# Moving the parameter work of an S5 branch and the rope table to the head of a fused mixer, and GpSimd's arithmetic there to VectorE

## The chip, the cores and the metric

The kernel runs on one core of a Trainium2 chip. A core has TensorE (PE, matrix products and transposes), VectorE (DVE), ScalarE (ACT), GpSimd (POOL) and the queue engine SyncE (SP), which here issues nearly all loads. The engines run side by side and wait for each other through semaphores. The metric is the device time of one execution in microseconds (us); lower is better.

## The reference

One transformer layer on 512 tokens of width 1024, in float32: a mixer of two branches, a cross attention to a memory, and a mixture of experts with 64 experts. The change is in the mixer alone:

```python
proj = x @ w_in
h_q, h_kv, k_rope_raw, u, g_mla, g_s5 = split(proj)
# S5 branch: per group g (32 groups, 64 states, 16 channels) a diagonal complex recurrence
dt = exp(log_dt); abar = exp(a * dt); bbar = ((abar - 1) / a) * b        # complex, from parameters alone
x_t = abar * x_{t-1} + bbar @ u_t;  y_t = Re(c @ x_t) + d * u_t
y_s5 = val * sigmoid(gate),  val, gate = split(gelu(y) @ w_glu)
# latent attention: q, k, v from rms_norm(h_q), rms_norm(h_kv), rope with cos/sin(positions * inv_freq)
merged = sigmoid(g_mla) * y_mla + sigmoid(g_s5) * y_s5
```

Everything that the S5 branch needs of `a`, `b`, `c` and `log_dt` (powers of `abar`, `bbar`, the step matrices) and the rope table `cs` depends on no product with x.

## The kernel before

float32 products are computed as three products of the engine's rounded float32 form: each operand is split into a high part (a cast by ACT, line 167) and a remainder (a subtraction, line 168, by DVE or by an engine that is passed in), and `mm3` issues high x high, high x low and low x high (L201 to L203). A weight of 128x2048 goes through `load` (a DMA on SP into one of two raw buffers), and `split`. Names: `wu0`, `wu1` are the two halves of u's weight, `wg00` to `wg31` those of the four gate blocks; a trailing r, h or l is the raw, high or low tile.

The front of the kernel, up to the first value product `pvv` of the attention, runs in this order of the code:

- x and `wqkv` are loaded; x is transposed (`xT`) and split; the latents `pl` = x @ wqkv; their mean squares and a Newton iteration on DVE (`ms`, `rms`, L306 and L210 to L219); the scaled latents (`lat`) are transposed (`cT`).
- `pu` = u, then transposed (`uT`). The S5 parameters: `nat`, `ldt`, `braw`, `cn` are loaded, `s5p` transposed, a long chain of small DVE operations on 128x16 tiles (`sp`, `pw`, `ap`, `bb`), the transposes `cstT` and `cst`. The rope table: `posi`, `ang`, `cs`.
- For four quarters Q: `factors` computes the step matrices `wi` on DVE, copied into `bd`, transposed into `im` (`imT`), the product `pkc`, and `pv`. Then the scan `vv` (`advance`, L608 to L611, on DVE), its carry `zz`, `factors` for the output matrices `om` (on POOL), and the correction of `vv` (L641, L642: on DVE, on POOL for Q = 3), then `py`, `yT`.
- Between these, the gate products `pg` run on PE as its filler; then `pq`, `pgl` and `pvv`.

A scheduler orders each engine's instructions by the position in the code, with the gate weights' splits advanced by a fixed offset, and each engine runs its list strictly in that order. Each DMA on SP also waits until the DMA eight places before it has landed, and buffers of one tag (the three `m2` buffers, the two raw weight buffers) are reused in turn.

The places that the change touches read, before:

```python
wu = w_cols(O_U, "wu")                    # the loads of u's weight; behind them, in the code, the loads of nat, ldt, braw, cn
w = factors(Q, 1, cst, -1, f"om{Q}", G)   # G is POOL, V is DVE
E = G if Q == 3 else V
wg = w_cols(c0, f"wg{i}", G if i in (0,3) else V)
G.tensor_copy(z[:, k, :, 96:112], z[:, k, :, 80:96].bitcast(F32))
```

Of the kernel before, what the change touches and what calls it, by code (L numbers as in the profile page):

```python
# [21 lines left out]
P = 128  # L22
# [79 lines left out]
def layer(ctx, tc, x, mem, positions, w_in, q_norm_g, kv_norm_g, w_uq, w_ukv, w_mla_o,  # L102
# [127 lines left out]


# [27 lines left out]
    c2_stack, cf_stack, cq_stack = ExitStack(), ExitStack(), ExitStack()  # L259
    c2p = c2_stack.enter_context(tc.tile_pool(name="c2p", bufs=1, side="right"))  # L260
    cfp = cf_stack.enter_context(tc.tile_pool(name="cfp", bufs=1, side="right"))
    mla = cq_stack.enter_context(tc.tile_pool(name="mla", bufs=1))
    identb = mla.tile([P, P], BF16, name="identb")
    V.tensor_copy(identb, ident)
    causal = mla.tile([P, P], BF16, name="causal")
    G.memset(causal, 0.0)
    G.affine_select(out=causal, in_=causal, compare_op=OP.is_ge, fill=-BIG, base=0,
                    pattern=[[-1, P]], channel_multiplier=1)

# [3 lines left out]
    rows = cfp.tile([P, 512], F32, tag="m2", bufs=3, name="rows")[:20, :P]  # L273
    r0 = 0
    COL = {}
    for nm, a in (("q", q_norm_g), ("kv", kv_norm_g), ("mg", mem_ln_g), ("mb", mem_ln_b)):
        n = a.shape[1] // P
        nc.sync.dma_start(rows[r0:r0 + n, :], a[0].rearrange("(r c) -> r c", c=P))
        COL[nm] = r0
        r0 += n  # L280
# [10 lines left out]
    wq = []
    for q_, r in enumerate(wqr):
        h, l = hilo(f"wqkv{q_}", (4, 512))
        split(h, l, r)
        wq.append((h, l))
    ssq = const.tile([P, NT, 2], F32, name="ssq")
    pls = four("pl")
    project(wq, pls, lambda i, k, h, l: (xh[:, k, cols_of(i)], xl[:, k, cols_of(i)]), whole)
    for t in range(NT):
        pl = pls[t]  # L300
        c = cfp.tile([P, 512], F32, tag="m2", bufs=3, name=f"lat{t}")
        for j in range(2):
            S.activation(c[:, j * 256:(j + 1) * 256], pl[:, j * 256:(j + 1) * 256], AF.Square,
                         accum_out=ssq[:, t, j:j + 1])
        ms = const.tile([P, 2], F32, tag="ms", bufs=2, name=f"ms{t}")
        V.tensor_scalar(ms, ssq[:, t, :], 1.0 / 256, None, OP.mult)  # L306
        rs = rsqrt(f"rms{t}", ms, RMS_EPS)
        for j in range(2):
            S.activation(c[:, j * 256:(j + 1) * 256], pl[:, j * 256:(j + 1) * 256], AF.Copy, scale=rs[:, j:j + 1])
        tp = trp(f"cT{t}")  # L310
        for k in range(4):
            PE.transpose(tp[:, k * P:(k + 1) * P], c[:, k * P:(k + 1) * P], ident)
        for k in range(4):
            g = col("q", k) if k < 2 else col("kv", k - 2)
            S.activation(cf[:, k, cols_of(t)], tp[:, cols_of(k)], AF.Copy, scale=g)

    s5k = ExitStack()
    s5 = s5k.enter_context(tc.tile_pool(name="s5", bufs=1))


    ujs = s5.tile([P, 2 * GI, STEP, 16], F32, tag="uy", name="ujs")
    wu = w_cols(O_U, "wu")
# [69 lines left out]
    tmpc = s5.tile([P, 4 * GI * 2], F32, name="tmpc")  # L392
# [113 lines left out]
    krr = load(w_inv[:, :, O_KR:O_KR + ROPE], "krr", (KD, ROPE))  # L506
    krw = ring.tile([P, 2048], F32R, tag="whi", bufs=2, name="krw")[:, :KD * P].rearrange("p (a b) -> p a b", a=KD)
    split(krw[:, :, 64:96], krw[:, :, 0:32], krr)
    for a, b in ((96, 80), (112, 64), (32, 16), (48, 0)):
        V.tensor_copy(krw[:, :, a:a + 16], krw[:, :, b:b + 16].bitcast(F32))  # L510
    pk = aux("pk")
    for k in range(KD):
        PE.matmul(pk, krw[:, k, :], xh[:, k, :], start=(k == 0), stop=False)
        PE.matmul(pk, krw[:, k, :], xl[:, k, :], start=False, stop=(k == KD - 1))
    kr = mla.tile([P, T], F32, name="kr")
    kr2 = cfp.tile([P, T], F32, tag="m2", bufs=3, name="kr2")
    S.copy(kr[h64], pk[0:64])
    V.tensor_tensor(kr[h64], pk[h64], kr[h64], OP.add)
    V.tensor_tensor(kr[h64], kr[h64], cs[h64], OP.mult)
    S.copy(kr2[64:96], kr[96:128])  # L520
    S.copy(kr2[96:128], kr[64:96])
    V.tensor_tensor(kr[h64], kr[h64], kr2[h64], OP.add)
    dump("kr", kr[h64])
# [32 lines left out]
    for Q in range(4):  # L556
# [30 lines left out]

        for c in range(2):
# [6 lines left out]
    tpz = s5.tile([P, 1024], F32, tag="tpz", name="tpz")  # L595
    zz = s5.tile([P, 2, GI, NJ], F32, name="zz")
# [24 lines left out]
    ys = s5.tile([P, STEP, 2 * GI, 16], F32, tag="uy", name="ys")  # L621
    pys = []
    for Q in range(4):
        qs = slice(Q * QG, (Q + 1) * QG)

        w = factors(Q, 1, cst, -1, f"om{Q}", G)
        om = ims[Q].rearrange("p c g (b s h) -> p c g b s h", b=2, h=16)
        for b, r in enumerate(halves):
            for c in range(2):
                (S.copy if b else G.tensor_copy)(om[r, c, :, b], w[r, c])  # L630
    for Q in (3, 0, 1, 2):
        qs = slice(Q * QG, (Q + 1) * QG)
        E = G if Q == 3 else V
        f = (bd.rearrange("p a b c d e -> p (a b c d e)") if Q == 3 else tpz)[:, :QG * NJ * n1]
# [1239 lines left out]
```

## Time and profile before

| | us |
|---|---|
| median of 3 runs | 1239.87 (1239.36 to 1240.43) |
| profiled execution | 1243.18, of which the span 1241.4 |
| PE busy | 1177.9 (95% of the span) |
| DVE busy | 900.2 (73%) |
| ACT busy | 726.6 (59%) |
| POOL busy | 329.3 (27%) |
| first `pvv` on PE | 244.09 after the span's start |

A row of the trace has a start or a count, the engine, the line of the kernel, the operation, its output and inputs, and durations; in square brackets or behind `<-` stands what the engine waited for before it. The profiled execution is 3.3 us above the median of the runs; a difference worked out on its rows is taken off the median.

### The profile page before, as it was taken

To read this page: it belongs to the slowest core of one execution; us is meant where nothing else is said; L and a number is where in the kernel's file an instruction comes from. 1 tells how busy PE (TensorE), PEld (TensorE's weight loads), DVE (VectorE), ACT (ScalarE), POOL (GpSimd) and SP (SyncE) were. 2 spreads that over 40 slices of the span, in tenths; PEclk is the share of its full clock that TensorE was granted. 3 is DMA by queue.
4 is the path that set the end of the run, shared out by engine and by line. 5 is a ranking of instruction groups with operands and counts; after the bars stand their busy time and mean duration, and the time that the engine had idled before them with its cause. 6 is when DMAs were issued, how large, how long until landed. Compare 5 with 4: busy or idle time off the path is not lost. (4 is left out here: it accounts for less than half of the span.)

```text
span 1241.4 us, 16244 instructions
## 1 busy us (share of the span) xinstructions
PE 1177.9 (95%) x5556; PEld 847.2 (68%) x5556; DVE 900.2 (73%) x1654; ACT 726.6 (59%) x1221; POOL 329.3 (27%) x280
## 2 busy tenths in 40 slices
PE   7979977899999899999999999999999999999995
PEld 6968866666678787846666666666666666666663
DVE  4588898446756854677778778788787887876785
ACT  3435413544525444424677777777777777776774
POOL 1020735230011243022122322224243232423321
PEclk9989988899999999999999999999999999999998
DMA  6522121121233257347999999999999999999975
GB/s 212 153 77 74 39 94 51 53 68 34 69 136 102 92 188 271 138 183 273 330 366 357 352 370 356 362 357 356 361 365 362 339 366 355 364 357 354 362 257 136
DMA packets 77596, 294.59 MB, mean 237 GB/s; under 512 B 18574, under 2 KB 22722, under 8 KB 52937
## 3 DMA queue, kind: packets, MB, share of 16 engines
q1 hardware_dynamic: 61592, 252.85, 55.1%
q0 software_dynamic: 15920, 40.69, 13.3%
q8 instruction: 44, 0.72, 0.2%
q14 instruction: 40, 0.32, 0.1%
HBM read 276.88 MB, written 32.77 MB: 249 GB/s over the span
## 5 line engine op out<-in xcount | busy, mean ns | idle before, releaser
L1252 POOL DMA_INDIRECT xg<-x2d,idx x64 | 74.0, 1157 | 384.9 <-PE xgT L1270 327.7
L1319 POOL DMA_INDIRECT ysum<-y,idx x62 | 123.1, 1985 | 91.2 <-ACT y L1331 63.2
L201 PE MATMUL pd<-edhl,hTh 128*96 128x512 f32 x124 | 98.4, 794 | 0.0
L1331 ACT ACTIVATE y<-pd,ws 96x512 f32<-96x512 f32 x124 | 78.6, 685 | 9.1 <-PE pd L203 9.1
L1314 PE MATMUL pd<-ed,hT 128*96 128x512 f32 x152 | 77.7, 593 | 0.5 <-PE psd L1531 0.5
L167 ACT CAST xgh<-xgT 128x384 fp32r<-128x384 f32 x128 | 60.3, 480 | 28.7 <-PE xgT L1270 28.6
L1270 PEld LDWEIGHTS xgT<-ident,xg 96*128 96x128 f32 x512 | 70.1, 215 | 7.0 <-issue 1.6
L1270 PE MATMUL xgT<-ident,xg 96*128 96x96 f32 x512 | 72.3, 283 | 1.9 <-DMA xg<-x2d,idx 1.4
L168 DVE TENSOR_TENSOR xgl<-xgT,xgh 128x384 fp32r<-128x384 f32 x128 | 65.0, 548 | 3.6 <-ACT xgh L167 3.6
L167 ACT CAST hTh<-hT 128x96 fp32r<-128x96 f32 x62 | 14.7, 238 | 73.3 <-PE hT L1293 73.3
L168 DVE TENSOR_TENSOR edhl<-ed,edhl 128x1024 fp32r<-128x1024 f32 x38 | 46.4, 1222 | 15.4 <-ACT edhl L167 15.3
L203 PE MATMUL pd<-edhl,hTl 128*96 128x512 f32 x124 | 49.4, 399 | 0.0
L1314 PE MATMUL pd<-edgx,hT 128*96 128x512 f32 x96 | 49.1, 592 | 0.0
L202 PE MATMUL pd<-edhl,hTh 128*96 128x512 f32 x124 | 48.6, 392 | 0.0
L202 PEld LDWEIGHTS pd<-edhl,hTh 128*96 128x96 f32 x124 | 20.2, 163 | 33.0 <-issue 33.0
L201 PEld LDWEIGHTS pd<-edhl,hTh 128*96 128x96 f32 x124 | 20.1, 162 | 33.0 <-issue 33.0
L167 ACT CAST edhl<-ed 128x1024 fp32r<-128x1024 f32 x38 | 39.4, 1037 | 3.8 <-DVE eg11l L168 3.8
L1228 DVE TENSOR_TENSOR oneh<-iota,posh 128x512 f16<-128x512 f16 x64 | 40.4, 681 | 0.1
L168 DVE TENSOR_TENSOR edhl<-edgx,edhl 128x1024 fp32r<-128x1024 f32 x24 | 29.3, 1222 | 10.7 <-ACT edhl L167 10.7
L1303 ACT COPY hT<-hT 128x96 f32<-128x96 f32 x62 | 14.8, 238 | 36.7 <-DVE hTl L168 36.7
L737 DVE TENSOR_REDUCE sm<-ps 128x1 f32<-128x128 f32 (+3 forms) x32 | 15.6, 488 | 23.8 <-PE ps L750 23.1
L665 ACT ACTIVATE sg<-pg 128x512 f32<-128x512 f32 x16 | 9.5, 596 | 36.6 <-PE pg L203 36.5
(1761 smaller groups left out, 3713.4 us busy)
## 6 DMA issues: line engine op xcount, KB each, us to landing
ed<-in_w_exp_down_dram SPq DMA_DIRECT2D x39, 1024.0 KB, 20.4
edgx<-in_w_exp_down_dram SPq DMA_DIRECT2D x25, 1024.0 KB, 13.7
x<-in_x_dram SPq DMA_DIRECT2D x4, 512.0 KB, 7.9
wqkvr<-in_w_in_dram SPq DMA_DIRECT2D x2, 1024.0 KB, 8.6
ysum<-zero SPq DMA_DIRECT2D x1, 2048.0 KB, 10.2
xr<-in_x_dram POOLq DMA_DIRECT2D x4, 512.0 KB, 5.0
wxv<-in_w_xkv_dram SPq DMA_DIRECT2D x2, 1024.0 KB, 6.5
eg3z<-in_w_exp_gu_dram SPq DMA_DIRECT2D x2, 1024.0 KB
```

Source lines behind the costliest of these rows:

```text
L167: a = S.copy(h, src)
L168: b = (eng or V).tensor_tensor(l, src, h.bitcast(F32), OP.subtract)
L201: PE.matmul(o, lh, rh, start=start, stop=False)
L202: PE.matmul(o, lh, rl, start=False, stop=False)
L203: PE.matmul(o, ll, rh, start=False, stop=stop)
L737: V.tensor_reduce(st[:, 0:1], ps, AX.X, OP.max)
L1228: V.tensor_tensor(oh_, iota.unsqueeze(1).to_broadcast([P, NT, P]), posn.to_broadcast([P, NT, P]), OP.is_equal)
L1252: return G.indirect_dma_start(out=xg, out_offset=None, in_=x2d[:, :], in_offset=bass.IndirectOffsetOnAxis(ap=ix, axis=0), bounds_check=T - ...
L1270: m_ = PE.transpose(tp[:, k * CAP:(k + 1) * CAP], xg[:CAP, 512 * z + k:512 * (z + 1):4], ident[:CAP, :CAP])
L1314: PE.matmul(po, f, wf[:, 0, c], start=True, stop=False)
L1319: marks["scatter"] = G.indirect_dma_start(out=ya[:, :], out_offset=bass.IndirectOffsetOnAxis(ap=ix, axis=0), in_=y, in_offset=None, bounds ...
L1331: S.activation(o, po, AF.Copy, scale=w)
```

## The change

Three things, all ahead of `pvv`:

- The loads of the S5 parameters and of the positions go right behind those of x and wqkv, ahead of u's weight. The parameters' arithmetic, the rope table and the step matrices `wi`, `imT`, `pkc` stand in the code ahead of u, the parameters and the rope table even ahead of the latents.
- POOL's arithmetic in the front goes to DVE: the low parts of wg0 and wg3, `om` and its copies, the correction for Q = 3 (which now comes last instead of first) and eight casts of `wuq`. POOL keeps memsets there.
- Pools and tags move with it (`cn` and `tpz` share the tag of `bd`, `im0` and `im1` get tiles of their own, `vv`, `U` and `ys` a new pool).

```diff
+    rows = cfp.tile([P, 512], F32, tag="m2", bufs=3, name="rows")[:20, :P]
...
+    nat = s5.tile([P, 4, P], F32, tag="fac", name="nat")[:GI]
+    nc.sync.dma_start(nat[:, 0, :], s5_a_re[0].rearrange("(a b) p -> a (b p)", b=2))
...
+    nc.sync.dma_start(braw[:, 0], s5_b_re[0].rearrange("(a b) p h -> (b p) a h", b=2))
+    nc.sync.dma_start(braw[:, 1], s5_b_im[0].rearrange("(a b) p h -> (b p) a h", b=2))
+    cns = []
...
+        nc.sync.dma_start(cn[:, :, 0, :], v)
...
+    nc.sync.dma_start(posi[h64], positions[0:1, :].to_broadcast([64, T]))
     xh = Halves(keep, "big", "xh")
...
-    cf = cfp.tile([P, 4, T], F32, name="cf")
...
-    wu = w_cols(O_U, "wu")
...
     S.activation(cs[h64], ang[h64], AF.Sin)
     dump("cs", cs[h64])
+    cf = cfp.tile([P, 4, T], F32, name="cf")
...
+    wu = w_cols(O_U, "wu")
...
+    for Q in range(4):
+        qs = slice(Q * QG, (Q + 1) * QG)
+        w = factors(Q, 0, bb, 1, f"wi{Q}", V)
...
+    pu = four("pu")
+    project(wu, pu, lambda i, k, h, l: (xh[:, k, i::STEP], xl[:, k, i::STEP]), whole)
...
-        w = factors(Q, 1, cst, -1, f"om{Q}", G)
+        w = factors(Q, 1, cst, -1, f"om{Q}", V)
...
-                (S.copy if b else G.tensor_copy)(om[r, c, :, b], w[r, c])
-    for Q in (3, 0, 1, 2):
+                (S.copy if b else V.tensor_copy)(om[r, c, :, b], w[r, c])
+    for Q in range(4):
...
-        E = G if Q == 3 else V
+        E = V
...
-            wg = w_cols(c0, f"wg{i}", G if i in (0,3) else V)
+            wg = w_cols(c0, f"wg{i}", V)
...
-            G.tensor_copy(z[:, k, :, 96:112], z[:, k, :, 80:96].bitcast(F32))
-            G.tensor_copy(z[:, k, :, 112:128], z[:, k, :, 64:80].bitcast(F32))
+            V.tensor_copy(z[:, k, :, 96:112], z[:, k, :, 80:96].bitcast(F32))
+            V.tensor_copy(z[:, k, :, 112:128], z[:, k, :, 64:80].bitcast(F32))
```

SP, from the last load of wqkv's small companions to the first gate weight, before (`ysum` is a 2 MB fill with zeros of a buffer that the experts add into; `krr` the weight of the rope key):

```order
L278 DMA rows<-in_mem_ln_b_dram 8x128
L156 DMA wu0r<-in_w_in_dram 128x4x512
L156 DMA wu1r<-in_w_in_dram 128x4x512
L333 DMA nat<-in_s_a_re_dram 16x128
L334 DMA nat<-in_s_a_im_dram 16x128
L336 DMA ldt<-in_s_log_dt_dram 16x2
L426 DMA braw<-in_s_b_re_dram 128x16x16
L427 DMA braw<-in_s_b_im_dram 128x16x16
L442 DMA cn_554<-in_s_c_re_dram 128x4x64
L799 DMA ysum_1839<-zero 4096x1x128
L156 DMA krr<-in_w_in_dram 128x8x32
L156 DMA wg00r<-in_w_in_dram 128x4x512
```

The same stretch of SP in the changed kernel:

```order
L278 DMA rows<-in_mem_ln_b_dram 8x128
...
L273 DMA braw<-in_s_b_re_dram 128x16x16
L274 DMA braw<-in_s_b_im_dram 128x16x16
L281 DMA cn<-in_s_c_re_dram 128x4x64
L281 DMA cn<-in_s_c_im_dram 128x4x64
L285 DMA posi<-in_positions_dram 64x512
L808 DMA ysum_1842<-zero 4096x1x128
L156 DMA wu0r<-in_w_in_dram 128x4x512
L156 DMA wu1r<-in_w_in_dram 128x4x512
L156 DMA krr<-in_w_in_dram 128x8x32
L156 DMA wg00r<-in_w_in_dram 128x4x512
```

The two loads of u's weight now stand behind the parameters, the positions and the 2 MB fill, which kept its place relative to the parameters.

DVE around the low part of u's first weight half and the first iteration on the latents' mean squares, before:

```order
L337 COPY nat<-ldt 16x128
L168 TENSOR_TENSOR wu0l<-wu0r,wu0h 128x2048
L306 TENSOR_SCALAR ms_290<-ssq 128x2
L443 COPY cn_554<-cn_554 128x4x64
L306 TENSOR_SCALAR ms_319<-ssq 128x2
L210 TENSOR_SCALAR rms_292<-ms_290 128x2
L210 TENSOR_SCALAR rms_321<-ms_319 128x2
```

The same place in the changed kernel, down to the same first step of the iteration:

```order
L168 TENSOR_TENSOR wu0l<-wu0r,wu0h 128x2048
L332 COPY sp<-s5p 128x48
L428 TENSOR_SCALAR cst<-cstT_323 64x256 x2
...
L428 TENSOR_SCALAR cst<-cstT_331 64x256 x2
...
L455 CAST ang<-posi 64x512
L336 TENSOR_SCALAR sp<-sp 128x16
L460 TENSOR_SCALAR phase<-rope_cols 128x1
L483 TENSOR_SCALAR ms_498<-ssq 128x2
L456 TENSOR_SCALAR ang<-ang,rope_cols 64x512
L337 SCALAR_TENSOR_TENSOR sp<-sp 128x16
L210 TENSOR_SCALAR rms_500<-ms_498 128x2
```

Between the split of wu0 and the end of that iteration (`rms_500`) there now stand the parameters' first chain and the rope table's operations, one between the other; before, the split was followed by the iteration alone.

DVE at the end of the correction of `vv`, where `yTz` is the split of the transposed S5 output, before:

```order
L641 TENSOR_TENSOR tpz<-ap,zz 128x448
L642 TENSOR_TENSOR vv<-vv,tpz 128x4x112
L168 TENSOR_TENSOR wukvl<-wukv,wukvh 128x512 x4
L168 TENSOR_TENSOR yTz_1739<-yT_1740,yTz_1738 128x8x16
L168 TENSOR_TENSOR yTz_1739<-yT_1753,yTz_1738 128x8x16
```

The same in the changed kernel:

```order
L650 TENSOR_TENSOR tpz<-ap,zz 128x448
L651 TENSOR_TENSOR vv<-vv,tpz 128x4x112
L168 TENSOR_TENSOR wukvl<-wukv,wukvh 128x512
L168 TENSOR_TENSOR yTz_1741<-yT_1742,yTz_1740 128x8x16
L650 TENSOR_TENSOR tpz<-ap,zz 128x448
L168 TENSOR_TENSOR yTz_1741<-yT_1755,yTz_1740 128x8x16
L168 TENSOR_TENSOR yTz_1741<-yT_1742,yTz_1740 128x8x16
L651 TENSOR_TENSOR vv<-vv,tpz 128x4x112
```

The correction of the last quarter now alternates with the splits of the first quarters' outputs on DVE, where before all of DVE's corrections were done when these began.

## Rows read from the trace of the kernel before

**Rows 1.** The page's head.
```profile
span 1241.4 us, 16244 instructions
```

**Rows 2.** What PE waited for from 0 to 262 us: line, releaser, us in total, times, longest.
```profile
PE pg L203 <- DVE wg21l L168: 9.0, 1, 9.0
PE py L650 <- DVE vv L642: 6.7, 2, 6.2
PE uT L469 <- DVE cst L449: 6.0, 1, 6.0
...
PE yT L674 <- DVE yTz L168: 3.4, 1, 3.4
PE pq L201 <- ACT cT L167: 1.4, 1, 1.4
PE uT L469 <- DVE U L470: 1.1, 1, 1.1
PE pq L202 <- DVE cT L168: 0.9, 1, 0.9
```

**Rows 3.** Stretches of the span: its limits and length, busy us of PE, PEld, DVE, ACT and POOL (with instructions), the granted TensorE clock as a share of full speed, the DMA engines' busy share, GB/s.
```profile
70.00:80.00 10.00, 2.84 (x11) 2.29 (x11) 9.36 (x18) 1.51 (x3) 4.79 (x2) 0.71 0.65 210
80.00:90.00 10.00, 10.00 (x38) 7.85 (x37) 7.92 (x44) 1.22 (x2) 0.00 (x0) 0.78 0.08 29
160.00:170.00 10.00, 6.56 (x23) 5.32 (x24) 9.83 (x13) 0.60 (x1) 0.63 (x1) 0.69 0.54 181
190.00:200.00 10.00, 6.77 (x33) 5.93 (x33) 9.69 (x11) 0.60 (x1) 8.00 (x8) 0.66 0.00 0
220.00:230.00 10.00, 6.87 (x19) 5.12 (x20) 6.09 (x10) 6.52 (x12) 1.73 (x3) 0.54 0.01 2
700.00:800.00 100.00, 100.00 (x477) 67.91 (x475) 80.06 (x106) 76.70 (x122) 25.20 (x20) 1.00 1.02 365
```

**Rows 4.** PE in order of time: start, us, line, operation.
```profile
37.78 0.60 PE L201 MATMUL pu<-wu0h,xhz 128*128 128x512 f32 x1
...
244.09 0.39 PE L201 MATMUL pvv<-wukvh,cT 128*128 128x512 f32 x1
```

**Rows 5.** POOL in order of time: start, us, line, operation, and in brackets its idle time before it.
```profile
70.27 4.52 POOL L168 TENSOR_TENSOR wg01l<-wg01r,wg01h 128x2048 fp32r<-128x2048 f32 x1
...
155.74 4.89 POOL L168 TENSOR_TENSOR wg30l<-wg30r,wg30h 128x2048 fp32r<-128x2048 f32 x1 [2.66 <-ACT wg30h L167]
```

**Rows 6.** DVE in order of time, beside these.
```profile
70.38 4.44 DVE L325 TENSOR_SCALAR sp<-sp 128x16 f32<-128x16 f32 x1
...
156.20 4.98 DVE L610 TENSOR_TENSOR tpz<-tpz,vv 128x512 f32<-128x512 f32 x1
161.10 2.28 DVE L168 TENSOR_TENSOR wg21l<-wg21r,wg21h 128x2048 fp32r<-128x2048 f32 x1
...
195.19 0.63 DVE L641 TENSOR_TENSOR tpz<-ap,zz 128x448 f32<-128x448 f32 x1
```

**Rows 7.** DVE from 60 to 211 us, grouped by line and shape: count, busy us, mean ns of one, idle before.
```profile
L610 DVE TENSOR_TENSOR tpz<-tpz,vv 128x512 f32<-128x512 f32 x7 | 12.7, 1810 | 0.0
L642 DVE TENSOR_TENSOR vv<-vv,tpz 128x448 f32<-128x448 f32 x12 | 9.8, 816 | 0.3
L641 DVE TENSOR_TENSOR tpz<-ap,zz 128x448 f32<-128x448 f32 x12 | 9.8, 813 | 0.4
L608 DVE TENSOR_TENSOR tpz<-ap,vv 128x512 f32<-128x512 f32 x7 | 8.7, 1238 | 0.2
...
L608 DVE TENSOR_TENSOR tpz<-ap,zz 128x32 f32<-128x32 f32 x14 | 7.3, 521 | 0.5
...
L611 DVE TENSOR_TENSOR zz<-tpz 128x32 f32<-128x32 f32 x14 | 3.0, 216 | 0.5
...
L329 DVE SCALAR_TENSOR_TENSOR ang<-posi,ang 64x512 f32<-64x512 f32 x3 | 2.1, 685 | 0.1
...
L549 DVE TENSOR_TENSOR wi<-pw,bb 128x256 f32<-128x256 f32 x4 | 1.7, 422 | 1.1 <-ACT bd L562 1.1
...
L357 DVE SCALAR_TENSOR_TENSOR sp<-sp 128x16 f32<-128x16 f32 x6 | 1.0, 175 | 0.1
```

**Rows 8.** SP's DMA issues in order of time: start, us of issuing.
```profile
12.96 0.41 SPq L156 DMA_DIRECT2D wu0r<-in_w_in_dram  x1
...
30.53 0.65 SPq L799 DMA_DIRECT2D ysum<-zero  x1
32.81 3.97 SPq L156 DMA_DIRECT2D krr<-in_w_in_dram  x1
```

**Rows 9.** DMA issues up to 60 us: count, KB each, median us from issue to landing.
```profile
ysum<-zero SPq DMA_DIRECT2D x1, 2048.0 KB, 10.2
wu0r<-in_w_in_dram SPq DMA_DIRECT2D x1, 1024.0 KB, 5.2
...
krr<-in_w_in_dram SPq DMA_DIRECT2D x1, 128.0 KB, 8.3
```

**Rows 10.** Two short stretches, columns as in Rows 3: the first lies on the parameter loads (64 byte pieces), the second on the fill with zeros.
```profile
28.00:31.50 3.50, 3.50 (x17) 2.89 (x16) 2.43 (x5) 2.64 (x5) 1.38 (x5) 1.00 0.83 96
31.50:35.00 3.50, 3.50 (x17) 2.89 (x16) 3.50 (x23) 0.94 (x5) 0.00 (x0) 1.00 1.00 275
```

**Rows 11.** ACT at the last cast of the latents' weight: start, us, and in brackets what it waited for.
```profile
13.65 1.90 ACT L167 CAST wqkv1h<-wqkvr 128x2048 fp32r<-128x2048 f32 x1 [2.07 <-DMA wqkvr<-in_w_in_dram]
```

More of the change, by code (lines that the diff above doesn't have):

```diff
@@ L229, in layer @@
     G.memset(one1, 1.0)
+    c2_stack, cf_stack, cq_stack = ExitStack(), ExitStack(), ExitStack()
+    c2p = c2_stack.enter_context(tc.tile_pool(name="c2p", bufs=1, side="right"))
+    cfp = cf_stack.enter_context(tc.tile_pool(name="cfp", bufs=1, side="right"))
+    mla = cq_stack.enter_context(tc.tile_pool(name="mla", bufs=1))
+    identb = mla.tile([P, P], BF16, name="identb")
+    V.tensor_copy(identb, ident)
+    causal = mla.tile([P, P], BF16, name="causal")
+    G.memset(causal, 0.0)
+    G.affine_select(out=causal, in_=causal, compare_op=OP.is_ge, fill=-BIG, base=0,
+                    pattern=[[-1, P]], channel_multiplier=1)
+    s5k = ExitStack()
+    s5 = s5k.enter_context(tc.tile_pool(name="s5", bufs=1))
     mix_stack = ExitStack()
@@ L257, in w_cols @@
         return [weight(w_inv[:, 4 * q:4 * q + 4, c0:c0 + 512], f"{name}{q}", (4, 512), None, eng) for q in range(2)]
[L259 to L268, printed above, removed]
     def c2(name, dt=F32):
         return c2p.tile([P, T], dt, tag="c2", bufs=16, name=name)
[L273 to L280, printed above, removed]
+    s5u = s5k.enter_context(tc.tile_pool(name="s5u", bufs=1))
     tp = trp("rowst")
@@ L287, in col @@
         return cols[:, COL[nm] + k:COL[nm] + k + 1]
-    cf = cfp.tile([P, 4, T], F32, name="cf")
[L291 to L321, printed above, removed]
-    wu = w_cols(O_U, "wu")
     def reduce_angle(ang, k, turn):
@@ L390, in layer @@
     V.tensor_tensor(q(CO_I), q(T1), q(DEN), OP.mult)
[L392 removed]
+    tmp3 = s5.tile([P, GI * 16], F32, name="tmp3")
+    tmpc = tmp3
     def cmul(eng, o_r, o_i, a_r, a_i, b_r, b_i, shape, t):
@@ L503, in layer @@
     dump("cs", cs[h64])
[L506 to L523, printed above, removed]
+    cf = cfp.tile([P, 4, T], F32, name="cf")
+    wq = []
+    for q_, r in enumerate(wqr):
+        h, l = hilo(f"wqkv{q_}", (4, 512))
+        split(h, l, r)
+        wq.append((h, l))
@@ new lines, in layer @@
+    ssq = const.tile([P, NT, 2], F32, name="ssq")
+    pls = four("pl")
+    project(wq, pls, lambda i, k, h, l: (xh[:, k, cols_of(i)], xl[:, k, cols_of(i)]), whole)
+    for t in range(NT):
+        pl = pls[t]
+        c = cfp.tile([P, 512], F32, tag="m2", bufs=3, name=f"lat{t}")
+        for j in range(2):
+            S.activation(c[:, j * 256:(j + 1) * 256], pl[:, j * 256:(j + 1) * 256], AF.Square,
+                         accum_out=ssq[:, t, j:j + 1])
+        ms = const.tile([P, 2], F32, tag="ms", bufs=2, name=f"ms{t}")
+        V.tensor_scalar(ms, ssq[:, t, :], 1.0 / 256, None, OP.mult)
+        rs = rsqrt(f"rms{t}", ms, RMS_EPS)
+        for j in range(2):
+            S.activation(c[:, j * 256:(j + 1) * 256], pl[:, j * 256:(j + 1) * 256], AF.Copy, scale=rs[:, j:j + 1])
+        tp = trp(f"cT{t}")
+        for k in range(4):
+            PE.transpose(tp[:, k * P:(k + 1) * P], c[:, k * P:(k + 1) * P], ident)
+        for k in range(4):
+            g = col("q", k) if k < 2 else col("kv", k - 2)
+            S.activation(cf[:, k, cols_of(t)], tp[:, cols_of(k)], AF.Copy, scale=g)
@@ L586, in layer @@
                 nc.sync.dma_start(tzs[Q][b * 64 + sh:b * 64 + 64, b, s_], ks[b * 64:b * 64 + 64 - sh])
+    pu = four("pu")
+    project(wu, pu, lambda i, k, h, l: (xh[:, k, i::STEP], xl[:, k, i::STEP]), whole)
+    for s in range(STEP):
+        S.copy(ujs[:, :, STEP - 1 - s, :], pu[s].rearrange("p (g h) -> p g h", h=16))
+    U = s5u.tile([P, GI, NI, NJ], F32, name="U")
+    for n in range(4):
+        tp = trp(f"uT{n}")
+        for k in range(4):
+            gi = 4 * n + k
+            PE.transpose(tp[:, k * P:(k + 1) * P], ujs[:, 2 * gi:2 * gi + 2].rearrange("p a b c -> p (a b c)"), ident)
+        (S.copy if n % 2 else V.tensor_copy)(U[:, 4 * n:4 * n + 4].rearrange("p a i j -> p a j i"),
+                                             tp.rearrange("p (a j i) -> p a j i", a=4, i=NI))
+    krr = load(w_inv[:, :, O_KR:O_KR + ROPE], "krr", (KD, ROPE))
+    krw = ring.tile([P, 2048], F32R, tag="whi", bufs=2, name="krw")[:, :KD * P].rearrange("p (a b) -> p a b", a=KD)
+    split(krw[:, :, 64:96], krw[:, :, 0:32], krr)
+    for a, b in ((96, 80), (112, 64), (32, 16), (48, 0)):
+        V.tensor_copy(krw[:, :, a:a + 16], krw[:, :, b:b + 16].bitcast(F32))
+    pk = aux("pk")
+    for k in range(KD):
+        PE.matmul(pk, krw[:, k, :], xh[:, k, :], start=(k == 0), stop=False)
+        PE.matmul(pk, krw[:, k, :], xl[:, k, :], start=False, stop=(k == KD - 1))
+    kr = mla.tile([P, T], F32, name="kr")
+    kr2 = cfp.tile([P, T], F32, tag="m2", bufs=3, name="kr2")
+    S.copy(kr[h64], pk[0:64])
+    V.tensor_tensor(kr[h64], pk[h64], kr[h64], OP.add)
+    V.tensor_tensor(kr[h64], kr[h64], cs[h64], OP.mult)
+    S.copy(kr2[64:96], kr[96:128])
+    S.copy(kr2[96:128], kr[64:96])
+    V.tensor_tensor(kr[h64], kr[h64], kr2[h64], OP.add)
+    dump("kr", kr[h64])
+    vv = s5u.tile([P, 2, GI, NI + 1, NJ], F32, name="vv")
+    V.memset(vv[:, :, :, 0, :], 0.0)
+    for Q in range(4):
+        qs = slice(Q * QG, (Q + 1) * QG)
         for c in range(2):
```

63 lines of the change are left out of this document (27 added, 36 removed).

## The prediction

> **What bounds the kernel now.** I read the page's span first (1241.4 us [rows 1], the profiled execution 1243.18 us), then stretches of the span, PE's waits, and DVE and POOL beside each other. From 600 us to the end of the experts PE has no gap: 700 to 800 us shows 100.00 us busy at the full clock, with the DMA engines full too, 365 GB/s [rows 3]. The change touches nothing there, and PE's and ACT's lists from `pvv` on are the same in both kernels; so what the front saves, up to the first `pvv` at 244.09 us [rows 4], the end gets, unless the experts' weights can't come sooner (a rival below).
>
> In the front PE's gaps of over half a microsecond lie in three places and a tail [rows 2]: 6.0 + 1.1 us for `uT` (on `cst`, and `U` behind it), 9.0 us for wg21's low part, 6.7 us for `vv` at `py`, and then 3.4 + 1.4 + 0.9 us for `yT` and `pq`. All of them wait for DVE or what hangs on it. Behind each gap PE runs at the lower granted clock (1.2 of 2.4 GHz) for a while; the stretches show what that costs. Busy time times what the mean clock lacks to 1.00 is 2.84 x 0.29 + 10 x 0.22 = 3.0 us behind the first, 6.56 x 0.31 = 2.0 behind the second, 6.77 x 0.34 = 2.3 behind the third and 6.87 x 0.46 = 3.2 in the tail [rows 3]. So the three gaps cost 10.1 + 11.0 + 9.0 = 30.1 us, the tail 8.9.
>
> **Why DVE is late there.** While POOL subtracts wg01 (70.27 us, 4.52 long [rows 5]), a DVE operation on 128x16 takes 4.44 us, beginning 0.11 us behind it [rows 6]; its like takes 0.175 [rows 7]. While POOL subtracts wg30 (155.74, 4.89), a 512 wide product takes 4.98 [rows 5, 6]. That operation stands right ahead of the split of wg21 (161.10), for which PE waits. The 512 wide operations should cost what L329's cost, 0.685 us, and the 128x32 ones 0.216 [rows 7]. What they took beyond that: L610 12.7 - 7 x 0.685 = 7.9, L608 8.7 - 4.8 = 3.9, L608 on 128x32 7.3 - 14 x 0.216 = 4.3, L641 and L642 9.8 - 12 x 0.63 = 2.2 each, L325 4.3: together 24.8 us of DVE lost to POOL's arithmetic, in these groups alone.
>
> **POOL's work on DVE.** Four splits of 2.28 [rows 6] = 9.1 us; `om`, four times six operations on 128x256 at 0.42 and two copies of half the partitions, at most 0.42 each [rows 7], = 13.4 us at most; the last correction, eight operations on 128x448 at 0.63 [rows 6], = 5.0; eight casts of 128x128, between 0.175 and 0.42 each [rows 7], 1.4 to 3.4, taken as 1.7 since they are small. Sum 29 us against at least 24.8 saved: DVE's load is about what it was. What changes is where the loss stands: no operation of 0.7 us is stretched to five just when PE needs the next split.
>
> **The three gaps.** With `cst`, the parameters and the step matrices done before u, the first gap has no cause left. The second is one stretched operation (4.98) and a DVE list that was 24.8 us behind; the third the same list and its stretched corrections. I take all three as gone, -30.1 us, and put 1 us for new waits on gate splits in the middle, where DVE is nearly full (9.83 of 10 us in 160 to 170 [rows 3]); bounds 0 and 4.
>
> **The new stall ahead of u.** This is the price. The listing shows u's weight behind the parameter loads, the positions and the 2 MB fill on SP, and the DVE list behind wu0's split filled with the parameters' chain and the rope table before the iteration `rms_500`, without which PE can't begin `cT` and, behind it, `pu`.
> - SP's first `braw` waits for the second half of wqkv, landed at 13.65 [rows 11]. Two `braw` and two `cn`, 131 KB each, in 64 to 256 byte pieces: the stretch on these loads moved 96 GB/s with the engines 0.83 busy [rows 10], so 524 KB take 4.5 us. `posi`: 0.5. Now 18.7.
> - The fill: 2.1 MB at 275 GB/s [rows 10], 7.6 us. Now 26.3.
> - wu0: alone it landed 5.2 us after its issue [rows 9]; at 365 GB/s its bytes are 2.9 us of that. Issued early, its latency lies under the fill: it lands between 29.2 and 31.5, taken as 30.3. Before, it was issued at 12.96 [rows 8] and landed at 18.2, long before its cast.
> - ACT's cast 1.9 [rows 11], DVE's split 2.28: 34.5.
> - Then DVE's list to the end of `rms_500`: some 57 operations on 128x16 and less at 0.175 busy, which overlap where two chains alternate (taken as 0.12, 6.8 us; all in a row 10), ten on 64x512 (0.685 for L329's three, less for the simpler: 5 us, at most 6.9), four of `cst` at most 0.42 each, and wu1's split, 2.28. Sum 15.5, between 13 and 20. Now 50.
> - ACT's scaling of the latent, behind the sine of the rope table, and four transposes: 2 us. `pu` begins at 52 instead of 37.78 [rows 4].
>
> That is 14.2 us later, of which some 1.5 us are PE's transposes of the parameters, which only moved ahead. PE has nothing else in its list there, so 12.7 us are idle; the clock behind it costs about what it cost behind the old gaps (2.0 to 3.0): 2.4. Together +15.1. Queued behind the split of wu0 are all of DVE's later operations, but the parameters among them are needed only after `pu`.
>
> **How the loads share the engines.** `krr`, 128 KB, was issued at 32.81 [rows 8] and took 8.3 us [rows 9]: it landed at 41.1, just behind the fill, issued at 30.53 and landed at 40.7. So a load behind the fill comes after it. The Trainium skill says so too ("DMA: Bandwidth & Descriptors", section Queues, rings and completion order): on each DMA engine the descriptors of one issuing engine are consumed in the order of its ring. The trace agrees by these two landings. With strict order the stall is the 15.1 above; were the fill and wu0 to share the engines evenly, wu0 would land near 25 and the sum would be 5 us lower. I keep the order.
>
> **The tail.** All corrections of `vv` now stand on DVE, 5.0 us more, with the casts' 1.7, and the splits of `yT` between them, so that `py`, `yT` and `pq` wait one after the other. Against that stand 4.4 us of stretching gone from L641 and L642. The tail's 8.9 us become between 8.9 and 16; I take 15, near the upper end, since PE reaches `py` about 5 us earlier than before and has nothing else to do: +6.
>
> **Sum.** -30.1 + 1 + 15.1 + 6 = -8.0 us: the first `pvv` near 236. On the profiled execution 1235.2; the median of the runs lies 3.3 lower, so 1231.9.
>
> **Rivals.**
> - *The stall ahead of u eats it all.* One mechanism: the DVE list between wu0's split and `rms_500`. It decides when `pu` begins at 60, 8 us later than I have it: with all small operations in a row (+3.2), the 64x512 ones at 0.685 (+1.9), and wu0 at 31.5 (+1.2) it is 58.3; two or three further waits of that list on ACT's sine, the positions or `cstT` pass it. Time 1240 to 1248, taken as 1244. For it: this list is the sum's largest guess. Against: in the trace such chains alternate with little idle time (0.1 us before six of L357 [rows 7]).
> - *DVE becomes the bound in the middle.* 29 us come, and if only the four largest losses (7.9, 4.3, 4.3, 3.9 = 20.4) go away, DVE ends 9 us later, and the gates' splits or `vv` are late again: about 1240. Against: the stretched operations begin and end with POOL's.
> - *Smaller stall.* wu0 shares the engines with the fill, or the tail is unchanged because the stretching pays for it: 5 or 6 us less, both 11: 1221 to 1226.
> - *Hidden anyway.* The experts' weights move at 365 GB/s with the engines full [rows 3]. If that stream and not PE sets the pace, an earlier PE only finds it later: within 1239 to 1241. Against: PE, too, has no gap there.
>
> **How the numbers follow.** The sum as worked out (1227 to 1237) 0.50; smaller stall 0.17; the stall eats it 0.15; DVE the bound 0.08; hidden 0.10. A measurement here tells 0.2% (2.5 us) from nothing. Faster: the first two, and a little of the others, 0.69; within 0.2%: hidden, and the edges of DVE and of the stall, 0.17; slower 0.14. The likeliest is 1232, by itself 1227 to 1237; the range that leaves out no more than 2 in 10 goes from the middle of the smaller stall to the near half of the slower case, 1222 to 1243.
>
> **What would show it.** In the changed kernel's waits of PE, one long wait, `cT` or `pu` for the chain of DVE and ACT, 11 to 14 us near 39 to 52; no wait on wg21l, `cst` or `vv` of several us in the middle; DVE's L608 to L611 at 0.69 us each; wu0's cast at about 30 instead of 28.55; waits of 12 to 15 us, lower clock included, from `py` to `pq`; the first `pvv` near 236. The prediction is wrong if `pu` begins after 60, if wu0 lands before 26, if new waits on gate splits sum to over 5 us, or if the gain at `pvv` is not found at the end.

## The result

The changed kernel takes 1231.74 us (median of 20 runs, 1225.72 to 1240.60) against 1240.38 (20 runs, 1237.14 to 1247.67); the ratio is 0.9924, with a 95% interval of 0.9906 to 0.9943. The forecast was 1231.9, a gain of 8.0 us; the medians gain 8.6. The profiled execution takes 1230.09 us, 13.1 less than that of before; the first `pvv` begins at 233.5 instead of 244.09 [rows 4], 10.6 us earlier. Single executions of either kernel lie several us apart, so that the front's 10.6 us and the medians' 8.6 don't contradict each other. From the first `pvv` to the end the profiled executions of all twelve kernels below took between 995.6 and 1000.9 us.

What PE waits for up to 262 us in the changed kernel (columns as in [rows 2]):

```profile
PE cT L489 <- ACT lat L486: 15.2, 1, 15.2
...
PE py L659 <- DVE vv L651: 2.8, 1, 2.8
PE pq L201 <- ACT sgl L800: 1.4, 1, 1.4
PE py L657 <- ACT ys L662: 1.3, 1, 1.3
PE pq L201 <- ACT cT L167: 1.3, 1, 1.3
PE yT L683 <- ACT yTz L167: 1.2, 1, 1.2
PE pq L202 <- DVE cT L168: 0.8, 1, 0.8
PE yT L683 <- ACT ys L662: 0.7, 1, 0.7
```

The three gaps of [rows 2] (`uT`, wg21's low part, the 6.2 us at `py`) are gone, and one of 15.2 us stands ahead of `cT`. The stretches behind the waits, one in the middle that holds nothing but gate products, and one of the experts (columns as in [rows 3]):

```profile
50.00:60.00 10.00, 5.29 (x20) 4.87 (x21) 8.38 (x77) 8.08 (x26) 0.00 (x0) 0.63 0.15 59
...
160.00:170.00 10.00, 10.00 (x46) 8.29 (x45) 8.23 (x37) 2.91 (x4) 0.00 (x0) 1.00 0.27 80
...
200.00:210.00 10.00, 6.00 (x41) 5.60 (x40) 7.38 (x19) 4.29 (x12) 0.00 (x0) 0.88 0.31 104
210.00:220.00 10.00, 7.23 (x25) 5.52 (x24) 4.62 (x5) 5.67 (x8) 2.77 (x3) 0.67 0.00 0
220.00:230.00 10.00, 10.00 (x42) 7.62 (x41) 3.22 (x5) 4.63 (x7) 2.58 (x2) 0.93 0.31 107
...
700.00:800.00 100.00, 100.00 (x482) 68.28 (x481) 80.07 (x105) 76.25 (x122) 24.66 (x18) 1.00 1.01 363
```

The lower clock costs 5.29 x 0.37 = 2.0 us behind the stall and 0.7 + 2.4 + 0.7 = 3.8 in the tail; the experts' stretch reads as before. And DVE's scan and corrections, grouped as in [rows 7]:

```profile
L651 DVE TENSOR_TENSOR vv<-vv,tpz 128x448 f32<-128x448 f32 x16 | 10.0, 623 | 0.3
L617 DVE TENSOR_TENSOR tpz<-ap,vv 128x512 f32<-128x512 f32 x7 | 4.8, 692 | 0.5 <-ACT vv L602 0.3
...
L619 DVE TENSOR_TENSOR tpz<-tpz,vv 128x512 f32<-128x512 f32 x7 | 4.8, 685 | 0.0
...
L617 DVE TENSOR_TENSOR tpz<-ap,zz 128x32 f32<-128x32 f32 x14 | 3.0, 214 | 0.5
```

L610 (now L619) went from 1810 to 685 ns of mean, L608 on 128x32 (now L617) from 521 to 214 [rows 7]: none of these is stretched. POOL is not quite without arithmetic ahead of `pvv`: three copies of the rope key from 213.0 us on and the operations on the gates (`sg`) from 224.6 on stay with it, as they were before.

**The same gain read along one chain.** `py` needs the corrected `vv`, the correction needs the carry, the carry the scan, and the scan the last `pv`. Three times mark that chain: the first operation of the scan (first start of L608, now L617), the first corrected `vv` on DVE (first start of L642, now L651), and the first `pvv`. Before, by operation, count, durations (min/median/max in ns), and first to last start:

```profile
L642 DVE TENSOR_TENSOR vv<-vv,tpz x12: 610/626/1465, 189.8 to 210.4; 128x448 f32<-128x448 f32 x12
L608 DVE TENSOR_TENSOR tpz<-ap,vv x7: 691/693/3397, 135.1 to 169.3; 128x512 f32<-128x512 f32 x7
```

The same two in the changed kernel, and its `pvv`:

```profile
L651 DVE TENSOR_TENSOR vv<-vv,tpz x16: 617/624/626, 177.1 to 206.7; 128x448 f32<-128x448 f32 x16
L617 DVE TENSOR_TENSOR tpz<-ap,vv x7: 691/692/693, 135.5 to 155.9; 128x512 f32<-128x512 f32 x7
```
```profile
L201 PE MATMUL pvv<-wukvh,cT x8: 389/389/395, 233.5 to 238.3; 128*128 128x512 f32 x8
```

The scan begins at 135.5 instead of 135.1: all the work that was moved ahead of u brought it forward by nothing, although the first step matrix is copied into `bd` at 70.2 instead of 89.8. Scan and carry take 41.6 us instead of 54.7, and from there to `pvv` it is 56.4 instead of 54.3. In sum 0.4 - 13.1 + 2.1 = -10.6 us.

### The profile page after: what moved, and what is told of

The parts are those of the page before. It is cut to its first block, busy times and chain, and to the rows that moved or that the text cites. A ratio compares the mean times of both kernels' runs of the same rounds, so it can differ in the third digit from the quotient of the medians.

```text
span 1227.9 us, 16204 instructions
## 1 busy us (share of the span) xinstructions
PE 1173.8 (96%) x5556; PEld 846.0 (69%) x5556; DVE 890.5 (73%) x1707; ACT 726.7 (59%) x1219; POOL 267.2 (22%) x227
## 5 line engine op out<-in xcount | busy, mean ns | idle before, releaser
L1261 POOL DMA_INDIRECT xg<-x2d,idx x64 | 71.4, 1116 | 384.8 <-PE xgT L1279 326.1
L740 POOL COPY kh<-kr 64x512 f32<-64x512 f32 x8 | 5.9, 761 | 195.1 <-PE yT L683 173.6
```

The costliest lines, as they stand in the source:

```text
L1261: return G.indirect_dma_start(out=xg, out_offset=None, in_=x2d[:, :], in_offset=bass.IndirectOffsetOnAxis(ap=ix, axis=0), bounds_check=T - ...
```

## The experiments

| kernel | gate products ahead of the last `pv` | scan begins | first correction | first `pvv` | median, us | ratio to before (95%) |
|---|---|---|---|---|---|---|
| before | 153 | 135.1 | 189.8 | 244.1 | 1240.38 | |
| changed | 134 | 135.5 | 177.1 | 233.5 | 1231.74 | 0.9924 (0.9906 to 0.9943) |
| 1 POOL's work on DVE alone | 194 | 136.1 | 182.0 | 231.1 | 1228.73 | 0.9895 (0.9862 to 0.9927) |
| 2 moved code alone | 110 | 140.6 | 182.3 | 250.7 | 1250.31 | 1.0080 (1.0055 to 1.0104) |
| 3 latents first | 271 | 163.1 | 202.0 | 250.7 | 1247.19 | 1.0045 (1.0017 to 1.0073) |
| 4 fill behind u's weight | 134 | 134.0 | 175.6 | 232.6 | 1229.65 | 0.9900 (0.9867 to 0.9934) |
| 5 rope table behind | 182 | 139.0 | 180.9 | 231.8 | 1232.21 | 0.9935 (0.9912 to 0.9958) |
| 6 = 1, copies to ACT | 163 | 126.6 | 172.4 | 224.5 | 1224.94 | 0.9858 (0.9828 to 0.9888) |
| 7 = 1, unread POOL work | 194 | 142.5 | 193.4 | 243.4 | 1243.73 | 1.0013 (0.9992 to 1.0034) |
| 8 gate splits on POOL | 110 | 142.3 | 182.2 | 246.1 | 1240.69 | 1.0011 (0.9983 to 1.0039) |
| 9 = changed, copies to ACT | 123 | 136.2 | 177.9 | 233.7 | 1232.15 | 0.9936 (0.9916 to 0.9956) |
| 10 = 5, copies to ACT | 171 | 136.4 | 178.6 | 233.1 | 1227.97 | 0.9889 (0.9854 to 0.9924) |

The times of the scan, the correction and `pvv` are from one profiled execution each; where they lie within 2 us of each other the medians don't rank the kernels. Each ratio is against executions of the kernel before in the same session (medians 1240.38 to 1241.21), so it differs a little from the quotient of the medians.

The second column is counted in PE's rows: how many gate products `pg` stand in PE's list ahead of the last `pv`, on which the scan waits. All else that PE does ahead of it is the same in number in every kernel. The code order alone doesn't fix these lists: before and kernel 1, which have the same code order up to there, differ by 41, and 46 gate products fill 10 us (above), 0.22 us each. So most of these experiments change PE's list besides what they were made for. Free of that are kernel 7 against 1 and kernel 4 against the changed kernel, in which PE does the same things in the same order.

**1. POOL's work on DVE alone** (the kernel before, its code order kept, but for the correction for Q = 3, which comes last and uses the tile of the others).

```diff
-        w = factors(Q, 1, cst, -1, f"om{Q}", G)
+        w = factors(Q, 1, cst, -1, f"om{Q}", V)
...
-        E = G if Q == 3 else V
+        E = V
...
-            wg = w_cols(c0, f"wg{i}", G if i in (0,3) else V)
+            wg = w_cols(c0, f"wg{i}", V)
```

> The kernel before with only the second part of the change: POOL's arithmetic ahead of pvv (low parts of wg0 and wg3, om, the correction for Q = 3, the casts of wuq) on DVE; loads and code order as before. If POOL's arithmetic is what stretched DVE's operations, L608 to L611 on 128x512 take 0.69 us each, the 9.0 us wait on wg21l and the first 6 us wait on cst shrink to under 2 us, there is no stall ahead of pu (37.8 us), and the first pvv comes 8 to 18 us before 244.1, near where the whole change has it (233.5). If the moved code is what brings the gain, and DVE's additional 29 us only replace what the stretching cost, pvv stays within 3 us of 244.1.

PE's longest waits are now at `py`, and `pvv`, in the second fence, begins at 231.1:

```profile
PE py L650 <- DVE vv L642: 13.1, 5, 7.6
PE yT L674 <- ACT ys L653: 1.5, 2, 0.8
```
```profile
L201 PE MATMUL pvv<-wukvh,cT x8: 389/389/395, 231.1 to 235.9; 128*128 128x512 f32 x8
```

This edit alone brings 13.0 us at `pvv` and 11.8 in the medians; the whole change brings 10.6 and 8.6, with intervals that overlap. The first gap (`uT` on `cst`) and that on wg21 went without any code being moved. What had held `cst` up before are two stretched operations on 128x16, L368 and the L325 of [rows 6], ahead of it on DVE:

```profile
67.66 2.68 DVE L368 TENSOR_TENSOR sp<-sp 128x16 f32<-128x16 f32 x1 [2.73 <-ACT sp L372]
...
74.85 0.42 DVE L449 TENSOR_SCALAR cst<-cstT 64x256 f32<-64x256 f32 x1
```

The third gap did not go: at `py` PE waits 13.1 us instead of 6.7. And the scan begins no earlier than before (136.1), since the gaps' 10.1 us ahead of it are taken by 41 more gate products (9.0 us), which are missing behind it.

**2. The moved code alone** (the changed kernel, its four kinds of POOL work back on POOL; the correction for Q = 3 first again, its temporary in another tile).

> The changed kernel with POOL's arithmetic put back on POOL; loads and code order as in the change. If the gain comes from POOL's work on DVE and the moved code costs a stall ahead of u, the stall of 15 us at cT stays, DVE's operations are stretched again (several of 3 to 5 us on 128x512 or less), and pvv comes at 241 to 252, so the kernel is no faster than before. If the moved code alone brings the gain, pvv comes at 233 to 236.

PE's waits of this kernel:

```profile
PE cT L489 <- ACT lat L486: 15.2, 1, 15.2
PE py L660 <- DVE vv L652: 6.9, 2, 6.0
PE yT L684 <- DVE yTz L168: 5.0, 1, 5.0
PE imT L535 <- DVE bd L531: 4.2, 1, 4.2
```

The stall stands as in the changed kernel, the waits of the stretched list are back in new places, and `pvv` comes at 250.7, 6.6 us behind that of before. So the moved code costs 6.6 us at `pvv` with POOL's work in place (9.8 in the medians) and 2.4 without (233.5 against 231.1; 3.0 in the medians, where the intervals overlap).

**3. Latents first.** The block from `cf` to the scaled latents goes back ahead of the parameters' arithmetic, with the load of the positions behind it; the parameters' loads stay early.

> The changed kernel with the block of the latents back in front of the parameters' arithmetic in the code (and, with it, the load of the positions behind it); the parameters' loads stay early, POOL stays without arithmetic. The iteration on the mean squares then stands right behind wu0's split on DVE. Both theories expect the 15 us stall ahead of cT to go, pu at 38 to 43. If the stall is a plain loss of PE, pvv comes 12 to 17 us before 233.5, at 216 to 222. If the time of the stall is used by DVE, whose list then sets when py can run, the loss comes back as a wait of 8 us or more at py on vv, and pvv is no earlier than 228.

PE's longest wait, and in the second fence the scan:

```profile
PE py L659 <- DVE vv L651: 21.2, 5, 15.4
```
```profile
L617 DVE TENSOR_TENSOR tpz<-ap,vv x7: 684/691/693, 163.1 to 184.5; 128x512 f32<-128x512 f32 x7
```

The stall is gone (`pu` at 39.1) and the kernel is slower than before: the scan begins 27.6 us later than in the changed kernel, and 21.2 us of waits at `py` take the place of 15.2 at `cT`. While PE stood, DVE worked through the parameters; the stall was no plain loss. In this order DVE copies the first step matrix 22.2 us later; the second line is the changed kernel's:

```profile
L531 DVE COPY bd<-wi x8: 277/282/286, 92.4 to 122.6; 64x256 f32<-64x256 f32 x8
```
```profile
L531 DVE COPY bd<-wi x8: 277/282/286, 70.2 to 99.8; 64x256 f32<-64x256 f32 x8
```

PE's list puts gate products into that time, 271 ahead of the last `pv` instead of 134 (some 30 us). They are missing later, when PE waits at `py`.

**4. The fill behind u's weight.** The zeros are made from wu1's low part.

```diff
-    G.memset(zero, 0.0)
+    V.tensor_scalar(zero, wu[1][1][:, 0, :P].bitcast(F32), 0.0, None, OP.mult)
```

> The changed kernel, but the fill of ysum waits for the split of wu1 (its zeros are made from that tile times 0), so that both loads of u's weight go ahead of it. wu0 then lands at 23 to 25 instead of 31.3. If the stall ahead of cT is set by that landing, as the prediction has it, cT comes 5 to 7 us before 54.7 and pvv at 226 to 229. If it is set by what the DVE list waits for behind wu0's split (the rope columns, which PE transposes only at 38.5), cT comes 1 to 3 us earlier, and pvv at 230 to 233.

PE's wait, and in the second fence ACT's cast of wu0 (start and duration, us):

```profile
PE cT L489 <- ACT lat L486: 13.4, 1, 13.4
```
```profile
28.35 1.91 ACT L167 CAST wu0h<-wu0r 128x2048 fp32r<-128x2048 f32 x1 [2.06 <-PE pl L203]
```

In the changed kernel the same cast waits for the load:

```profile
31.39 1.91 ACT L167 CAST wu0h<-wu0r 128x2048 fp32r<-128x2048 f32 x1 [4.70 <-DMA wu0r<-in_w_in_dram]
```

With the load out of the way the cast is held by PE, which still reads the buffer it writes to, until 28.35, where it also stood before the change (28.55). The late landing can cost 3.0 us at most; 2.2 of them arrive at `cT` and 0.9 at `pvv`. The rest of the stall lies behind the split; experiment 5 shows where.

**5. The rope table behind the latents.** As in 3, but only from `inv_row` to `cs`, and the positions' load; the parameters stay ahead.

> The changed kernel with only the rope table (its columns, the positions' load and the angles) behind the block of the latents in the code; the S5 parameters and their arithmetic stay ahead of it, POOL stays without arithmetic. If the stall at cT comes from the rope table's operations in DVE's list and from the squares that wait for its buffers, the wait at cT falls from 15.2 to under 3 us, pu begins at 38 to 42, DVE does the parameters meanwhile, and pvv comes at 225 to 231. If the stall's length only shows when DVE is done with the parameters, as in the run with the latents first, py waits 10 us or more on vv and pvv comes at 235 or later.

PE's waits of this kernel:

```profile
PE py L659 <- DVE vv L651: 9.2, 5, 2.8
...
PE pg L201 <- ACT wg00h L167: 4.7, 1, 4.7
...
PE cT L457 <- ACT lat L454: 1.0, 1, 1.0
```

The rope table made the stall: without it ahead, `cT` waits 1.0 us and `pu` begins at 41.3 instead of 55.5. Of those 14 us, 1.7 are left at `pvv` (231.8), just outside what was expected, and the scan begins 3.5 us later: 48 more gate products stand ahead of the last `pv` (10.6 us), PE waits 4.7 us on wg00, and the lower clock behind that wait costs 2.7 (8.86 us busy from 70 to 80 at 0.70). At `py` PE then waits 9.2 us instead of 2.8.

**6. Kernel 1 with copies on ACT.** All evictions of `U`, `im` and `vv` and both halves of `bd` and `om` go to ACT.

```diff
-            (S.copy if c else V.tensor_copy)(vv[:, c, qs, 1:NI + 1, :], pv.rearrange("p (a i j) -> p a i j", a=4, i=NI))
+            S.copy(vv[:, c, qs, 1:NI + 1, :], pv.rearrange("p (a i j) -> p a i j", a=4, i=NI))
```

> The kernel of the first experiment (old code order, no POOL arithmetic), with five kinds of copies moved from DVE to ACT: both halves of bd and om, and all evictions of U, im and vv, about 12 us of DVE. If DVE's list is what py waits for there (13.1 us in five waits), the waits at py fall to 5 to 9 us in sum, and pvv comes 4 to 8 us before 231.1, at 223 to 227. If the waits come from the latency of the chain itself, or ACT's list becomes late instead, pvv stays within 2 us of 231.1.

PE's longest wait, and in the second fence the scan:

```profile
PE py L650 <- DVE vv L642: 8.4, 5, 2.3
```
```profile
L608 DVE TENSOR_TENSOR tpz<-ap,vv x7: 685/691/693, 126.6 to 151.3; 128x512 f32<-128x512 f32 x7
```

The scan begins 9.5 us earlier than in kernel 1, `pvv` 6.6. PE has no gap from 30 to 170 us in either kernel; the last `pv` comes 6.8 us earlier because 31 fewer gate products stand ahead of it. How much of the gain is DVE's shorter list and how much PE's other order is not separated. With 1224.94 us this version beats both kernels; its interval lies below that of the changed kernel.

**7. Kernel 1 with POOL work that nobody reads.**

```diff
+            if i in (0, 3):
+                with tc.high_priority(offset=AHEAD):
+                    for h, l in wg:
+                        for k in range(4):
+                            for e in range(2):
+                                G.tensor_tensor(scr, h[:, k, 0:256].bitcast(F32), h[:, k, 256:512].bitcast(F32), OP.mult)
```

> The kernel of the first experiment, with 32 products of 128x256 on POOL added whose results nobody reads, eight behind each high part of wg0's and wg3's weights, about as long as POOL's subtractions in the kernel before (5 us each). No other engine depends on them. If POOL's arithmetic stretches DVE by sharing something with it, DVE operations of 0.2 to 0.7 us take 0.8 to 5 us beside them, 8 to 20 us of DVE are lost in all, and pvv comes 4 to 15 us behind 231.1. If the stretching came from what waited for POOL's results, nothing is stretched and pvv stays within 1 us.

POOL's eight products behind wg30's high part (start, us):

```profile
152.02 16.53 POOL L668 TENSOR_TENSOR scr<-wg30h 128x256 f32<-128x256 f32 x8 [68.44 <-ACT wg30h L167]
```
The first of the eight, and the last:
```profile
152.02 6.92 POOL L668 TENSOR_TENSOR scr<-wg30h 128x256 f32<-128x256 f32 x1 [68.44 <-ACT wg30h L167]
...
167.49 1.07 POOL L668 TENSOR_TENSOR scr<-wg30h 128x256 f32<-128x256 f32 x1
```
DVE beside them:
```profile
151.97 2.27 DVE L168 TENSOR_TENSOR wg30l<-wg30r,wg30h 128x2048 fp32r<-128x2048 f32 x1
...
157.66 0.67 DVE L610 TENSOR_TENSOR tpz<-tpz,vv 128x512 f32<-128x512 f32 x1
158.37 1.11 DVE L611 TENSOR_TENSOR vv<-tpz 128x512 f32<-128x512 f32 x1
159.52 1.11 DVE L608 TENSOR_TENSOR tpz<-ap,vv 128x512 f32<-128x512 f32 x1
160.55 1.22 DVE L609 TENSOR_TENSOR tpz<-api,vv 128x512 f32<-128x512 f32 x1
```

Nothing waits for these products, and yet DVE's 0.68 us operations take 1.1 to 1.2 from 158.4 on, POOL's eight take 16.5 us in place of 5 (a product of this size took 0.64 in the kernel before), and `pvv` comes at 243.4, 12.3 us behind kernel 1: nearly all that moving POOL's work had brought. From 30 us on DVE does the same 449 operations in the same order in both kernels, up to `pvv`; in kernel 1 they are 170.7 us long in sum, here 184.0. The two engines hold each other up. The split of wg30, which began 0.05 us ahead of POOL's first product, kept its 2.27 us, and the nine operations behind it kept theirs. POOL's first product ended only when these were done; from then on operations of both engines are stretched.

**8. Only the gate splits back on POOL** (`G if i in (0,3) else V` for wg in the changed kernel).

> The changed kernel with only the low parts of wg0 and wg3 back on POOL (18.7 us of POOL), om, the correction and the casts stay on DVE. If the splits are most of what POOL's arithmetic cost, pvv comes at 239 to 245, more than half of the way from 233.5 to the 250.7 of the run with all of POOL's work back. If om and the correction cost more, pvv comes at 234 to 239.

`pvv` comes at 246.1, 12.6 of the 17.2 us between the changed kernel and kernel 2, just outside what was expected (245). By the medians it is 9.0 of 18.6. POOL's four long splits are about half of the harm, or more.

**9. The changed kernel with copies on ACT**, as in 6.

> The changed kernel with the same five kinds of copies moved from DVE to ACT as in the sixth experiment. If PE, once it has begun u after the stall, is itself the bound until py (no gap from 60 to 197 us in the changed kernel), DVE's 12 us less do nothing there and only the 2.8 us wait on vv in the tail can go: pvv at 230 to 233.5. If DVE's list is the bound of the changed kernel too, pvv comes 4 to 8 us earlier, at 225.5 to 229.5, as it did for the old code order (231.1 to 224.5).

PE's longest waits:

```profile
PE cT L489 <- ACT lat L486: 16.7, 1, 16.7
PE py L659 <- DVE vv L651: 3.8, 1, 3.8
```

`pvv` at 233.7, just outside what was expected and no gain: what brought 6.6 us in the old order brings nothing here. From 60 to 190 us PE has no gap in the changed kernel; there PE, late by the stall, is the bound, and DVE has room. (PE's list has 123 gate products ahead of the last `pv` here instead of 134; the stall is 1.5 us longer.)

**10. Kernel 5 with copies on ACT.**

> The kernel with the rope table behind the latents (no stall ahead of u, 9.2 us of waits on vv at py, 4.7 on wg00's high part), with the same copies moved from DVE to ACT. If without the stall DVE's list is what py waits for, the waits at py fall to 4 to 7 us and pvv comes 3 to 7 us before 231.8, at 225 to 229; the wait on wg00's high part, which ACT casts, stays or grows by up to 3. If ACT becomes the engine that is late, pvv stays at 230 to 233.

The waits on `vv` at `py` fell to 6.7 us, but those on ACT (`ys`) grew from 0.9 to 2.5, and `pvv` came at 233.1. The scan begins 2.6 us earlier than in kernel 5 and the time behind the first correction grew from 50.9 to 54.5. ACT's share in that was not taken apart. The median is 4.2 us below that of kernel 5, the other way round from `pvv`, and the intervals overlap: the runs don't show whether the copies' move helps here.

## Why the prediction was right, step by step

**The carry to the end: right.** 10.6 us at `pvv`, 8.6 in the medians, with the experts' stretch as before. Over all kernels the first `pvv` moves by 26.2 us (224.5 to 250.7) and what follows it by no more than 5.3 (995.6 to 1000.9); the rival by which the experts' weights hide the gain has fallen.

**The three gaps, -30.1 us: right in size, half right in cause.** None is left but 2.8 us at `py`, which are counted with the tail, and no new wait came in the middle (1 us was allowed). But the sentence that the first gap goes because `cst` and the parameters now come before u is not what the runs show: kernel 1 loses that gap with the old order, since the two operations that held `cst` up were stretched by POOL. The second went there too. The third was put down to the same stretched list, and that is not shown: kernel 1, with POOL's work on DVE, waits 13.1 us at `py`. In the changed kernel PE comes to `py` late by the stall; kernel 5, without the stall, waits 9.2 us there. So part of what the third gap gave back was paid for by the stall.

**POOL's effect on DVE: right.** Kernel 7 shows it without any dependence. A DVE operation beside one of POOL's long ones lasts about as long as that one: 4.44 us, begun 0.11 us behind one of 4.52 [rows 5, 6]. The Trainium skill describes it as a shared port pair ("SBUF — State Buffer", sections SBUF: two separate sides and Who interferes with whom): a lock that whichever engine starts first holds for its whole instruction, with DVE operations of two SBUF inputs (against GpSimd's reads only), or in a two-port mode, on the one side. These runs agree in both directions: a DVE operation begun behind POOL's long one lasted as long as that, and the split that began ahead of POOL's product was not touched, while the product of 0.64 us took 6.92. That the product waited for nine more operations behind the split is more than this rule says.

**The stall, +15.1 us: 17.2 measured** (15.2 and 2.0 of clock). The landing was well placed: wu0, issued at 18.43, lands at 31.3, behind the fill, which lands at 27.6 (30.3 was taken). `pu` begins at 55.5, 3.5 us later than forecast: the split of wu0 ends 1.1 us later, DVE's list behind it takes 16.7 us (15.5 were taken, with bounds of 13 and 20), and ACT with the transposes 3.2; the 2 us that were taken for these come from no row, and ACT's rows show a table load of 1.28 us ahead of the sine. One thing in this step was wrong, and kernel 4 shows it: the smaller stall was made 5 us cheaper, as if wu0, landed near 25, could be cast at once, while the row of the cast before (28.55) waited for PE. The order in which the loads stand behind the fill is real but is worth at most 3 us, and 0.9 at the end.

**The tail, +6: +3.0 measured.** Idle, with the 2.8 at `py`, 2.8 + 1.3 + 1.2 + 0.7 + 1.3 + 0.8 = 8.1 us and 3.8 of lower clock give 11.9 against 8.9; 15 was taken between 8.9 and 16. That the stretching which fell away from L641 and L642 paid for more of the added work than assumed would explain it; this was not tested.

So the sum held since the stall came out 2.1 us longer, the tail 3.0 shorter and the middle 1 shorter. That these differences nearly cancel, and that the median fell within 0.2 us of the forecast when the gain at `pvv` was 2.6 us larger, is luck. What the sum did not contain is how the two parts share the result. Its terms put 30.1 us to the credit of the whole change; in fact POOL's work on DVE brings 13.0 by itself, and the moved code brings nothing more beside it (2.4 us less at `pvv`). The parameters' new place brings the scan forward by nothing, because PE, which must make `pv` for it, has no gap from 60 us on and is behind by the stall; and without the stall (kernel 5) PE's list has more gate products ahead of `pv`. A sum over the gaps of one kernel can't show this; it takes each part of the change by itself.

## What to carry to other kernels

Elementwise work given to GpSimd is not free of VectorE even where nothing depends on it; its price is read from the durations of VectorE's operations beside it. Long operations (kernel 8) and short ones (kernel 7) both cost over 12 us at `pvv` here. When a change has two parts, follow the chain that decides (here last `pv`, scan, correction, `pvv`) as well as the gaps of the busy engine, and try each part alone: here the simple half was at least as good as the whole. A gap that an engine waits out is only worth what the next engine in the chain does not use it for. And before a gain is put down to an edit, compare the order in which the engines do their work: where a scheduler makes the lists, work that fills a gap early is missing later.

## What the runs showed of the hardware that was not expected

Two engines in conflict slow each other: eight POOL products that would take 5 us took 16.5 beside a dense DVE, the first of them 6.92, so that POOL's work was not even done at its own price. And with several short waits PE ran below the full clock for long: in kernel 1 the granted clock was 0.57 of full speed from 180 to 190 us, behind the 7.6 us wait at `py`, 0.92 and 0.83 in the two stretches of 10 us behind it, and 0.66 from 210 to 220.
